# The right operands of a seven-product down projection, formed during the up projection and kept in DRAM

## Chip, cores and metric

The kernel runs on one core of one Trainium2 chip. The metric is device time in microseconds: the median of three runs of the kernel is 1607.43 us (1604.57 to 1608.24). Lower is better.

## What is computed

One layer of an encoder over 1024 prompt tokens and 32 sample tokens: a modulated input projection, two groups of attention heads, an output projection with a norm, and then a feed-forward part with a norm. The change lies in the feed-forward part, which the reference writes as

```python
def _conv_ffn(u, conv_prev, w_up, conv_w, conv_b, w_down):
    T = u.shape[1]
    a, b = jnp.split(jnp.einsum('btd,df->btf', u, w_up), 2, axis=-1)
    a_pad = jnp.concatenate([conv_prev.astype(a.dtype), a], axis=1)
    conv = conv_b
    for j in range(CONV_WIDTH):
        conv = conv + a_pad[:, j:j + T] * conv_w[j]
    h = jax.nn.silu(conv) * b
    return jnp.einsum('btf,fd->btd', h, w_down), a_pad[:, -(CONV_WIDTH - 1):]
```

with u of 1024 features, h of 2816 (22 tiles of 128) and everything in float32.

## The kernel before

**Exact products.** TensorE multiplies float32r. `split` (L87 to L89) makes two float32r parts of a float32 tile: `hi` by a copy on ScalarE (ACT) and `lo`, the difference, on VectorE (DVE) or GpSimd (POOL). `mm3` (L82) then does three matmuls for one product.

**Up projection.** The loop over `j` (22 tiles of h) and `s` (gate half, plain half) takes 44 units. A unit loads 512 KB of `w_up` (`up_weights`, L868, on SyncE's queue, SP), splits it (tiles `wu`, two buffers each of raw, hi and lo), and does 144 matmuls of 352 columns into three accumulators. With `s == 0` ACT copies the accumulators to `row` and DVE does the convolution (L1129 to L1131) and ACT the SiLU; with `s == 1` DVE multiplies into `hT[j]` (L1137 to L1139). The buffers of `wu` are free for unit u + 2 when TensorE (PE) has done unit u. A generator `residuals` (L1081 to L1105), advanced once in each unit, turns the rows that the first norm left in DRAM into the residual of the second: SP loads a piece of `dx1`, POOL multiplies and adds, POOL stores it to `dres`; a piece has `RW` = 256 columns, so there are 36.

**Down projection.** h (1024 by 2816) times `w_down` (2816 by 1024) is done as a two by two block product with seven products of half size instead of eight (sums of blocks on both sides). Products are `i` = 0 to 6, each with 11 steps `k`, so 77 steps `n`; a step is 4 blocks of 128 tokens with 3 matmuls each of 128 by 512, and four of the products carry the 32 sample tokens with 2 more matmuls a step: 924 + 88 = 1012 matmuls. For a step the kernel does three things ahead: `load(n + 3)` brings one or two 256 KB tiles of `w_down`; `left(n)` sums tiles of h for later products; `prepare(n + 2)` forms the left operand (from h) and the right operand (from `w_down`), the sums mostly on POOL (L1198, L1211, L1216, L1218, L1220, L1226), and splits both into `hi` and `lo` (tiles `oh`, `ol`, four buffers, shared in turn by two pools). Both need DVE's subtraction on L89. In products 5 and 6 the finished rows get their gate and residual on POOL (L1258, L1259, 128 by 1024) and their norm on ACT and DVE.

**Order.** Most of this is ordered by the framework's scheduler. Each engine, and SP's queue, then takes its instructions strictly in that order.

Of the kernel before, what the change touches and what calls it, by code (L numbers as in the profile page):

```python
# [16 lines left out]
P = 128  # L17
# [10 lines left out]
TT = T + TS  # L28
# [7 lines left out]
RW = 256  # L36
# [17 lines left out]
def layer_kernel(ctx: ExitStack, tc: tile.TileContext, a: dict, o: list):  # L54
# [88 lines left out]
    dres = dp.tile([TT, D], F32, name="dres")  # L143

# [928 lines left out]
    hT = [hpool.tile([P, TT], F32, name=f"h{j}") for j in range(NJ)]  # L1073
    with pool("pe") as pe:
# [31 lines left out]
        resid = residuals()  # L1106
        for j in range(NJ):
            c = pe.tile([P, ROW], F32, name=f"cv{j}", tag="cv", bufs=1)
            for s in range(2):
                if j or s:  # L1110
                    next(resid, None)
# [40 lines left out]
    NK = NJ // 2  # L1152
# [3 lines left out]
    with pool("px") as px, pool("pf") as pf:  # L1156
# [10 lines left out]
        res, ready, raws_, rest = {}, {}, {}, []  # L1167
# [3 lines left out]

        def wq(fh, ch, k):
            return w_dn[:, fh * NK + k, ch * 512:(ch + 1) * 512]


        LOADS = [((1, 0), None), ((1, 1), None), ((0, 1), (0, 0)), ((0, 0), None), (None, (1, 1)), ((1, 1), (0, 1)), (None, (1, 0))]

        def load(n):
            if n >= NPH * NK:
                return  # L1180
            i, k = divmod(n, NK)
            raw = (px.tile if n % 3 == 2 else pw.tile)([P, 2, 512], F32, name=f"xt{i}{k}", tag="raw", bufs=1 if n % 3 == 2 else 2)
            x2 = None
            if LOADS[i][0]:
                nc.sync.dma_start(raw[:, 1], wq(*LOADS[i][0], k))
            if LOADS[i][1]:
                x2 = pt_(f"x2{i}{k}", "x2", 3, (P, 512))
                nc.sync.dma_start(x2, wq(*LOADS[i][1], k))
            raws_[n] = raw, x2

        def left(n):

            if n >= NPH * NK:
                return
            i, k = divmod(n, NK)
            if i == 0:
                nc.vector.tensor_tensor(xq[k], hq(0, 1, k), hq(1, 1, k), ALU.add)
                nc.gpsimd.tensor_tensor(xq[k], xq[k], hq(0, 0, k), ALU.subtract)  # L1198

        def prepare(n):  # L1200
# [4 lines left out]
            raw, x2 = raws_.pop(n)  # L1205
            pl = px if n % 4 < 2 else pw
            hi = pl.tile([P, 2, 512], F32R, name=f"oh{i}{k}", tag="wh", bufs=2)
            lo = pl.tile([P, 2, 512], F32R, name=f"ol{i}{k}", tag="wl", bufs=2)
            yk = hq(1, 0, k)
            if i == 1:  # L1210
                nc.gpsimd.tensor_tensor(raw[:, 0], hq(1, 0, k), xq[k], ALU.subtract)  # L1211
                split(hi, lo, raw)
            else:
                if i == 2:
                    nc.vector.tensor_tensor(raw[:, 0], hq(0, 1, k), hq(1, 1, k), ALU.add)
                    nc.gpsimd.tensor_tensor(yk, raw[:, 1], x2, ALU.subtract)  # L1216
# [20 lines left out]
            ready[n] = hi, lo  # L1237
# [153 lines left out]

    hp_.__exit__(None, None, None)
# [61 lines left out]
```

## Time and profile before

| | us |
|---|---|
| median of 3 runs | 1607.43 |
| the profiled execution, its own time | 1607.87 |
| span in the profile | 1606.1 |
| PE busy | 1493.1 (93%) |
| DVE busy | 884.0 (55%) |
| POOL busy | 563.9 (35%) |
| up projection, about | 784 to 1299 |
| down projection, first to last matmul, about | 1300 to 1578 |
| end after the last matmul | about 28 |

Busy time is the time in which an engine worked on an instruction; a matmul's end is modelled, so that PE's busy time is not PE at its peak. In the page's 40 slices the down projection is slices 33 to 39. A wait is put down to what ended it. The DMA share is the mean busy share of the core's 16 DMA engines; it can go a little over 1 where transfers of several queues overlap.

### The profile page before, as it was taken

The page shows a single profiled execution, that of the slowest core. Times are in us where ns is not written, and L with a number is a line of the kernel's source. Part 1 is how long each engine was busy: PE and PEld are TensorE (multiplying, and loading weights), DVE is VectorE, ACT ScalarE, POOL GpSimd, SP SyncE. Part 2 cuts the span into 40 slices and gives each one's busy share as a digit, 9 for nine tenths or more (in the row PEclk, how much of TensorE's full clock was granted, in tenths as well). Part 3 has the DMA queues.
Part 4 walks back from the last instruction along what each step waited for, and adds up shares of the span by engine and source line. Part 5 has one row for each costly group of instructions (what it writes and reads, how often), then busy time and mean ns, then how long its engine had stood idle before and what let it go on. Part 6 is the DMA issues. An engine that isn't in the chain of part 4 may idle for free.

```text
span 1606.1 us, 22667 instructions
## 1 busy us (share of the span) xinstructions
PE 1493.1 (93%) x8525; PEld 1242.7 (77%) x8525; DVE 884.0 (55%) x1621; ACT 575.5 (36%) x1176; POOL 563.9 (35%) x635
## 2 busy tenths in 40 slices
PE   6999999978999999899999999999999999999753
PEld 4677777745546777687899999999999987878542
DVE  4522336644446899467753243323332378797996
ACT  3211211245647787535532112111211134444321
POOL 0002014644413433124355650000000056583885
PEclk9999999999999999999999999999999999999977
DMA  9623411489653444335423331111111122543322
GB/s 267 164 94 110 130 47 69 146 235 255 179 179 91 122 108 95 137 133 208 143 76 108 105 109 51 53 40 53 40 53 40 40 80 87 168 154 116 133 81 78
DMA packets 177967, 183.86 MB, mean 114 GB/s; under 512 B 9121, under 2 KB 138178, under 8 KB 177858
## 3 DMA queue, kind: packets, MB, share of 16 engines
q1 hardware_dynamic: 167858, 151.00, 31.6%
q0 software_dynamic: 9424, 30.37, 6.4%
q8 instruction: 67, 1.10, 0.3%
q10 hardware_dynamic: 576, 1.05, 0.2%
q14 instruction: 42, 0.34, 0.1%
HBM read 147.62 MB, written 26.38 MB: 108 GB/s over the span
## 4 chain that ended last, share of the span: by engine, by line
PE 65%; DVE 12%; DMA 10%; POOL 5%; issue 4%; SPq 2%; ACT 2%; POOLq 0%; DVEq 0%; ACTq 0%
PE up L82 15%; PE upc L82 8%; PE wd L82 7%; PE wo L82 4%; DVE ol L89 3%; PE po L82 3%; PE Sf L82 2%; DMA dres<-rr 2%; PE ptf L116 2%; DMA rr<-dx 2%; PE Sd L82 2%; DMA adan<-in_w_ada 1%; PE pod L82 1%; DMA xt<-in_w_down 1%; POOL rr L1099 1%
## 5 line engine op out<-in xcount | busy, mean ns | idle before, releaser
L82 PE MATMUL wd<-ol,oh 128*128 128x512 f32 x308 | 119.9, 403 | 17.9 <-DVE ol L89 17.9
L82 PE MATMUL wd<-oh,ol 128*128 128x512 f32 x308 | 119.5, 403 | 6.8 <-DVE ol L89 6.7
L82 PE MATMUL wd<-oh 128*128 128x512 f32 x308 | 114.0, 397 | 4.9 <-ACT oh L88 2.4
L1127 POOL COPY cvo<-row 128x2 f32<-128x2 f32 x22 | 15.5, 706 | 277.2 <-ACT row L1125 277.2
L89 DVE TENSOR_TENSOR ol<-h,oh 128x512 fp32r<-128x512 f32 x77 | 80.9, 1064 | 25.3 <-ACT oh L88 24.9
L628 POOL TENSOR_SCALAR wf<-wf,rs 128x128 f32<-128x128 f32 (+7 forms) x64 | 47.4, 745 | 109.3 <-DVE rs L594 81.7
L82 PEld LDWEIGHTS wd<-ol,oh 128*128 128x128 f32 x308 | 59.3, 193 | 33.8 <-DVE ol L89 21.6
L82 PEld LDWEIGHTS wd<-oh,ol 128*128 128x128 f32 x308 | 59.6, 194 | 22.8 <-DVE ol L89 10.8
L82 PEld LDWEIGHTS wd<-oh 128*128 128x128 f32 x308 | 59.0, 192 | 19.5 <-ACT oh L88 2.8
L88 ACT CAST oh<-h 128x512 fp32r<-128x512 f32 x77 | 46.7, 618 | 70.9 <-PE wd L82 30.6
L1124 ACT COPY row<-up 128x352 f32<-128x352 f32 x44 | 17.8, 458 | 142.0 <-PE up L82 112.2
L1132 ACT ACTIVATE cv<-cv 128x1058 f32<-128x1058 f32 x22 | 24.0, 1089 | 103.5 <-DVE cv L1131 103.5
L89 DVE TENSOR_TENSOR ol<-xt,oh 128x512 fp32r<-128x512 f32 (+1 forms) x55 | 54.8, 999 | 8.2 <-ACT oh L88 8.2
L88 ACT CAST oh<-xt 128x512 fp32r<-128x512 f32 (+1 forms) x55 | 38.8, 707 | 54.7 <-PE wd L82 31.3
L593 ACT ACTIVATE wf<-wf,lo 128x128 f32<-128x128 f32 (+7 forms) x64 | 49.5, 776 | 23.4 <-DVE lo L590 21.5
L89 DVE TENSOR_TENSOR wh<-wr,wh 128x512 fp32r<-128x512 f32 x40 | 28.6, 738 | 51.2 <-ACT wh L88 51.2
L82 PE MATMUL po<-ptpf,vf 128*64 128x256 f32 (+1 forms) x320 | 54.8, 378 | 0.5 <-DVE ptpf L618 0.4
L88 ACT CAST wh<-wr 128x512 fp32r<-128x512 f32 x40 | 24.3, 621 | 86.0 <-DMA wr<-in_w_in 19.0
L593 ACT ACTIVATE wd<-wd,lo 128x128 f32<-128x128 f32 (+7 forms) x64 | 49.6, 777 | 13.0 <-DVE lo L590 11.0
L590 DVE CUSTOM_DVE_ANT_0 wf<-Sf,nb 128x512 f32<-128x512 f32 (+3 forms) x64 | 36.9, 588 | 31.1 <-PE Sf L82 19.7
L653 POOL TENSOR_SCALAR wd<-wd,rs,lam 128x128 f32<-128x128 f32 (+7 forms) x32 | 26.5, 827 | 63.0 <-DVE rs L594 57.8
L116 PE MATMUL ptf<-cst,wf 128*128 128x128 f32 x288 | 47.1, 284 | 1.1 <-POOL wf L628 0.7
(1542 smaller groups left out, 4823.2 us busy)
## 6 DMA issues: line engine op xcount, KB each, us to landing
xt<-in_w_down SPq DMA_DIRECT2D x55, 256.0 KB
x<-in_w_down SPq DMA_DIRECT2D x44, 256.0 KB
wr<-in_w_in SPq DMA_DIRECT2D x20, 512.0 KB
adam<-in_w_ada SPq DMA_DIRECT2D x32, 256.0 KB
adan<-in_w_ada SPq DMA_DIRECT2D x32, 256.0 KB
ga<-in_w_ada SPq DMA_DIRECT2D x16, 512.0 KB
out<-z POOLq DMA_DIRECT2D x12, 512.0 KB, 4.0
x<-in_x_prompt SPq DMA_DIRECT2D x8, 512.0 KB
```

The source lines that it names most:

```text
L82: nc.tensor.matmul(out, l, r, start=start, stop=stop, **k)
L88: nc.scalar.copy(hi, src)
L89: (eng or nc.vector).tensor_tensor(lo, src, f(hi), ALU.subtract)
L116: nc.tensor.transpose(out, in_, ident[:n, :n])
L590: nc.vector.tensor_tensor_reduce(w[:, c], S[:, 0:n], t, -1.0, lo, ALU.add, ALU.min, lo_)
L593: nc.scalar.activation(w[:, 0:ext], w[:, 0:ext], AF.Exp, bias=lo, scale=-1.0, accum_out=sm)
L628: nc.gpsimd.tensor_scalar(w, w, rs, 1.0, ALU.mult, ALU.mult)
L653: nc.gpsimd.tensor_scalar(e1, e1, r1, lam, ALU.mult, ALU.mult)
L1099: nc.gpsimd.tensor_tensor(r, r, gb[c0][0:n, 0], ALU.mult)
L1124: nc.scalar.copy(row[:, 2 + g * G3:2 + (g + 1) * G3], accs[g])
L1127: nc.gpsimd.tensor_copy(cvo[:, 0, :, j], row[:, T:T + 2])
L1132: nc.scalar.activation(c[:, 0:L], c[:, 0:L], AF.Silu)
```

## The change

The right operands of the seven products (sums of tiles of `w_down`, and their `hi` and `lo`) are formed by a generator during the first tiles of the up projection and stored to DRAM in `dwn` (154 tiles of 128 by 512, 40.4 MB). The down projection loads them ready made. The generator is advanced three times in each unit of `j` < 16; its tiles live where the last six tiles of h will be. The sums of h that POOL did go to DVE. The residual pieces get half as wide (128 columns, so 72), and two are taken per unit.

```diff
-RW = 256
+RW = 128
...
+    dwn = dp.tile([7 * NJ, P, 512], F32, name="dwn")
...
+    LENT = 6
+    hT = [hpool.tile([P, TT], F32, name=f"h{j}") for j in range(NJ - LENT)]
+    lent_ = pool("ln", "right")
...
+    def right_operands():
+        q = {}
+        def load(k, which):
+            for fh, ch in which:
+                q[k, fh, ch] = t = lent.tile([P, 512], F32, name=f"wq{k}{fh}{ch}", tag=f"wq{fh}{ch}", bufs=1)
+                nc.sync.dma_start(t, w_dn[:, fh * NK + k, ch * 512:(ch + 1) * 512])
+        late = []
+        def stored(due):
+            while late and (due is None or late[0][0] <= due):
+                _, i, k, hl = late.pop(0)
+                for p in range(2):
+                    nc.sync.dma_start(dwn[(i * NK + k) * 2 + p], f(hl[p]))
+        n = 0
+        load(0, ((0, 0), (0, 1), (1, 1), (1, 0)))
+        yield
+        for k in range(NK):
+            t = lent.tile([P, 512], F32, name=f"wt{k}", tag="wt", bufs=1)
+            for i, src in ((3, "00"), (2, "t1"), (5, "t3"), (4, "t2"), (1, "11"), (6, "t4"), (0, "10")):
+                stored(n - 2)
...
+                if src == "t1":
+                    nc.vector.tensor_tensor(t, q[k, 0, 1], q[k, 0, 0], ALU.subtract)
...
+                hl = [lent.tile([P, 512], F32R, name=f"wn{i}{k}{p}", tag=f"wn{p}", bufs=4) for p in range(2)]
+                split(hl[0], hl[1], x)
+                late.append((n, i, k, hl))
+                n += 1
+                yield
...
         for j in range(NJ):
+            if j == NJ - LENT:
+                for _ in operands:
+                    pass
+                lent_.__exit__(None, None, None)
...
-                if j or s:
+                for _ in range(2 if j or s else 0):
                     next(resid, None)
...
+                    if j < NJ - LENT:
+                        next(operands, None)
...
         def load(n):
...
+            hi = pl.tile([P, 2, 512], F32R, name=f"oh{i}{k}", tag="wh", bufs=2)
+            lo = pl.tile([P, 2, 512], F32R, name=f"ol{i}{k}", tag="wl", bufs=2)
+            for p, t in enumerate((hi, lo)):
+                nc.sync.dma_start(f(t[:, 1]), dwn[(i * NK + k) * 2 + p])
...
-                nc.gpsimd.tensor_tensor(xq[k], xq[k], hq(0, 0, k), ALU.subtract)
+                nc.vector.tensor_tensor(xq[k], xq[k], hq(0, 0, k), ALU.subtract)
...
-                split(hi[:, 1], lo[:, 1], r)
-                split(hi[:, 0], lo[:, 0], l)
-                if i == 3:
-                    nc.gpsimd.tensor_tensor(l, l, hq(0, 1, k), ALU.subtract)
+            split(hi[:, 0], lo[:, 0], l)
+            if i == 3:
+                nc.vector.tensor_tensor(l, l, hq(0, 1, k), ALU.subtract)
```

**DVE in the up projection**, from the split of the weights of `j` = 3 on (`wu30l`; `cv` is the convolution, `h` the product with the plain half). Before:

```order
L89 TENSOR_TENSOR wu30l_8424<-wu30r_8421,wu30h_8423 128x1024
L1129 TENSOR_SCALAR cv2_8227<-row2_8313,cvw_67,pcol_66 128x1058
L1130 SCALAR_TENSOR_TENSOR cv2_8227<-row2_8313,cvw_67,cv2_8227 128x1058
L1131 SCALAR_TENSOR_TENSOR cv2_8227<-row2_8313,cvw_67,cv2_8227 128x1058
L1137 TENSOR_TENSOR h2_7843<-up21_8337,cv2_8227 128x352 x2
L1138 TENSOR_TENSOR h2_7843<-upc21_8338,cv2_8227 128x320
```

and of the change (`wn` are the new operands, named by product, k and part; `wt` a sum of tiles of `w_down`):

```order
L89 TENSOR_TENSOR wu30l_8591<-wu30r_8588,wu30h_8590 128x1024
L1199 TENSOR_SCALAR cv2_8327<-row2_8443,cvw_67,pcol_66 128x1058
L89 TENSOR_TENSOR wn521_8546<-wq201_8350,wn520_8545 128x512
L1200 SCALAR_TENSOR_TENSOR cv2_8327<-row2_8443,cvw_67,cv2_8327 128x1058
L89 TENSOR_TENSOR wn421_8600<-wt2_8478,wn420_8599 128x512
L1201 SCALAR_TENSOR_TENSOR cv2_8327<-row2_8443,cvw_67,cv2_8327 128x1058
L1121 TENSOR_TENSOR wt2_8478<-wq210_8511,wt2_8478 128x512
L89 TENSOR_TENSOR wn121_8634<-wq211_8413,wn120_8633 128x512
L1207 TENSOR_TENSOR h2_7844<-up21_8476,cv2_8327 128x352 x2
L89 TENSOR_TENSOR wn621_8665<-wt2_8478,wn620_8664 128x512
L1208 TENSOR_TENSOR h2_7844<-upc21_8477,cv2_8327 128x320
```

The operands' subtractions and sums now stand between the convolution and the products, and the next split of `wu` behind them: from `wu30l` to `wu90l` there are 56 of the 77 steps, so 9.3 in each `j`, and the last of the 77 stands just ahead of `wu91l`.

**SP's queue** at the same place, from the load of `wu30r` on. Before:

```order
L868 DMA wu30r_8421<-in_w_up 128x8x128
L1091 DMA rr05_8419<-dx1_83 128x256
L1091 DMA rr06_8517<-dx1_83 128x256
L1091 DMA rr07_8607<-dx1_83 128x256
L1091 DMA rr08_8705<-dx1_83 32x256
L868 DMA wu31r_8519<-in_w_up 128x8x128
```

and of the change, its first rows:

```order
L869 DMA wu30r_8588<-in_w_up 128x8x128
L1095 DMA dwn_85<-wn000_8138 128x512
L1095 DMA dwn_85<-wn310_8169 128x512
L1095 DMA dwn_85<-wn601_8107 128x512
L1095 DMA dwn_85<-wn001_8139 128x512
L1087 DMA wq110_8230<-in_w_down 128x512
L1095 DMA dwn_85<-wn311_8170 128x512
L1087 DMA wq200_8348<-in_w_down 128x512
L1095 DMA dwn_85<-wn210_8233 128x512
L1151 DMA rr04_8213<-dx1_83 128x128
```

Between the loads of `wu30r` and `wu31r` there are 19 transfers now, where there were four; every store among them is queued behind those ahead of it and waits for the ACT or DVE result that it stores.

**DVE in the down projection**, from the second step of product 4 on. Before:

```order
L89 TENSOR_TENSOR ol41_13146<-h12_7853,oh41_13145 128x512
L89 TENSOR_TENSOR ol41_13146<-xq0_12003,oh41_13145 128x512
L89 TENSOR_TENSOR ol42_13182<-h13_7854,oh42_13181 128x512
L1373 TENSOR_TENSOR ya0_11995<-ya0_11995,wd30_12888 128x512
L89 TENSOR_TENSOR ol42_13182<-xq1_12004,oh42_13181 128x512
```

and of the change:

```order
L89 TENSOR_TENSOR ol41_13852<-xq0_12812,oh41_13851 128x512
L89 TENSOR_TENSOR ol42_13872<-xq1_12813,oh42_13871 128x512
L1420 TENSOR_TENSOR ya0_12804<-ya0_12804,wd30_13640 128x512
```

Of the two subtractions of a step one is left.

## Rows read from the trace of the kernel before

**Rows 1.** The page's head and part 1: busy time of the engines.
```profile
span 1606.1 us, 22667 instructions
...
PE 1493.1 (93%) x8525; PEld 1242.7 (77%) x8525; DVE 884.0 (55%) x1621; ACT 575.5 (36%) x1176; POOL 563.9 (35%) x635
```

**Rows 2.** Busy time by stage: window, PE, PEld, DVE, ACT, POOL, PEclk, DMA, GB/s.
```profile
1299.00:1342.00 43.00, 40.30 (x170) 30.73 (x168) 39.14 (x51) 16.22 (x38) 35.95 (x16) 1.00 0.32 105
...
784.00:1299.00 515.00, 511.07 (x3200) 508.60 (x3199) 186.07 (x234) 111.29 (x181) 114.06 (x207) 1.00 0.22 66
1299.00:1472.00 173.00, 167.28 (x723) 134.17 (x722) 146.23 (x186) 75.39 (x156) 102.88 (x59) 1.00 0.40 133
1472.00:1579.00 107.00, 79.97 (x299) 58.87 (x297) 106.14 (x111) 28.95 (x53) 83.35 (x42) 0.89 0.29 101
1579.00:1606.10 27.10, 0.00 (x0) 0.00 (x0) 13.73 (x28) 3.15 (x4) 18.75 (x17) 0.58 0.22 82
```

**Rows 3.** The chain that ended last, in order of time: start, us, what.
```profile
1276.34 7.63 PE up L82 x48
1283.97 3.81 PE upc L82 x24
...
1299.85 1.21 DVE ol L89 x2
...
1342.17 19.58 PE wd L82 x85
...
1413.04 58.82 PE wd L82 x258
```

**Rows 4.** Waits of PE from 1298 us on: us in total, times, longest.
```profile
PE wd L82 <- DVE ol L89: 24.6, 13, 9.8
```

**Rows 5.** Groups of instructions from 1298 us on: busy us, mean ns, idle before.
```profile
L1218 POOL TENSOR_TENSOR h<-x,h 128x512 f32<-128x512 f32 x22 | 38.0, 1744 | 1.8 <-DMA x<-in_w_down 1.6
L1198 POOL TENSOR_TENSOR xq<-xq,h 128x512 f32<-128x512 f32 x11 | 28.7, 2642 | 5.6 <-DVE xq L1197 5.6
L89 DVE TENSOR_TENSOR ol<-xt,oh 128x512 fp32r<-128x512 f32 x44 | 39.7, 903 | 2.8 <-ACT oh L88 2.8
```

**Rows 6.** Groups of DVE from 1470 to 1580 us, the same columns.
```profile
L89 DVE TENSOR_TENSOR ol<-h,oh 128x512 fp32r<-128x512 f32 x32 | 36.9, 1185 | 0.0
L1274 DVE TENSOR_TENSOR ya<-ya,lng 128x1024 f32<-128x1024 f32 x4 | 8.2, 2055 | 0.0
```

**Rows 7.** Tile ol: duration ns min/median/max, first and last start us.
```profile
L89 DVE TENSOR_TENSOR ol<-h,oh x77: 668/684/2875, 1288.3 to 1568.8; 128x512 fp32r<-128x512 f32 x77
```

**Rows 8.** Tile yb on POOL, the same columns.
```profile
L1259 POOL TENSOR_TENSOR yb<-yb,rs x4: 2497/2808/2835, 1552.8 to 1569.3; 128x1024 f32<-128x1024 f32 x4
L1315 POOL TENSOR_TENSOR yb<-yb,lnb x4: 1257/1260/1265, 1592.8 to 1601.6; 128x512 f32<-128x512 f32 x4
```

**Rows 9.** Tile wu100h, the weights of unit j = 10, s = 0.
```profile
L82 PE MATMUL up<-u2h,wu100h x16: 320/323/325, 1024.3 to 1031.5; 128*128 128x352 f32 x16
...
L89 DVE TENSOR_TENSOR wu100l<-wu100r,wu100h x1: 1225/1225/1225, 1014.0 to 1014.0; 128x1024 fp32r<-128x1024 f32 x1
```

**Rows 10.** Busy time in stretches of interest for the DMA, columns as in rows 2.
```profile
20.00:60.00 40.00, 35.07 (x254) 23.28 (x253) 23.27 (x46) 16.53 (x28) 0.00 (x0) 1.00 1.08 282
1362.00:1413.00 51.00, 48.19 (x207) 38.25 (x205) 41.32 (x49) 22.80 (x46) 32.36 (x21) 1.00 0.52 171
1395.00:1405.00 10.00, 10.00 (x45) 7.89 (x43) 8.85 (x6) 4.33 (x8) 9.78 (x7) 1.00 0.61 199
194.00:198.00 4.00, 4.00 (x19) 3.31 (x18) 1.98 (x3) 2.14 (x4) 0.00 (x0) 1.00 1.03 397
1000.00:1200.00 200.00, 200.00 (x1260) 200.00 (x1259) 63.64 (x78) 38.61 (x62) 11.20 (x34) 1.00 0.16 46
940.00:960.00 20.00, 18.20 (x101) 17.34 (x100) 6.42 (x7) 3.90 (x7) 12.68 (x23) 0.91 0.44 131
```

**Rows 11.** SP's queue at the start of the up projection: start, us, what.
```profile
788.44 0.37 SPq L868 DMA_DIRECT2D wu11r<-in_w_up  x1
```

More of the change, by code (lines that the diff above doesn't have):

```diff
@@ L1072, in layer_kernel @@
     hpool = hp_.__enter__()
-    hT = [hpool.tile([P, TT], F32, name=f"h{j}") for j in range(NJ)]
+    NK = NJ // 2
+    LENT = 6
+    hT = [hpool.tile([P, TT], F32, name=f"h{j}") for j in range(NJ - LENT)]
+    lent_ = pool("ln", "right")
+    lent = lent_.__enter__()
+    def right_operands():
[17 more added lines that the diff above has]
+                stored(n - 2)
+                if k + 1 < NK:
+                    if i == 1:
+                        load(k + 1, ((0, 0), (0, 1)))
+                if k and i == 2:
+                    load(k, ((1, 0),))
+                if i == 0 and k + 1 < NK:
+                    load(k + 1, ((1, 1),))
+                if src == "t1":
+                    nc.vector.tensor_tensor(t, q[k, 0, 1], q[k, 0, 0], ALU.subtract)
+                    x = t
+                elif src == "t3":
+                    x = q[k, 0, 1]
+                    nc.vector.tensor_tensor(x, q[k, 1, 1], x, ALU.subtract)
+                elif src == "t2":
+                    nc.vector.tensor_tensor(t, q[k, 1, 1], t, ALU.subtract)
+                    x = t
+                elif src == "t4":
+                    nc.vector.tensor_tensor(t, q[k, 1, 0], t, ALU.subtract)
+                    x = t
+                else:
+                    x = q[k, int(src[0]), int(src[1])]
+                hl = [lent.tile([P, 512], F32R, name=f"wn{i}{k}{p}", tag=f"wn{p}", bufs=4) for p in range(2)]
[3 more added lines that the diff above has]
+                yield
+        stored(n - 2)
+        yield
+        stored(None)
@@ L1106, in layer_kernel @@
         resid = residuals()
+        operands = right_operands()
         for j in range(NJ):
+            if j == NJ - LENT:
+                for _ in operands:
+                    pass
+                lent_.__exit__(None, None, None)
+                hp2_ = pool("h2", "right")
+                hpool2 = hp2_.__enter__()
+                hT += [hpool2.tile([P, TT], F32, name=f"h{i}") for i in range(j, NJ)]
             c = pe.tile([P, ROW], F32, name=f"cv{j}", tag="cv", bufs=1)
             for s in range(2):
-                if j or s:
+                for _ in range(2 if j or s else 0):
                     next(resid, None)
@@ L1151, in layer_kernel @@
     psum("psd", m=6, po=1, ms=1)
-    NK = NJ // 2
     NPH = 7
@@ L1181, in load @@
             i, k = divmod(n, NK)
[L1182 to L1189, printed above, removed]
+            pl = px if n % 4 < 2 else pw
+            hi = pl.tile([P, 2, 512], F32R, name=f"oh{i}{k}", tag="wh", bufs=2)
+            lo = pl.tile([P, 2, 512], F32R, name=f"ol{i}{k}", tag="wl", bufs=2)
+            for p, t in enumerate((hi, lo)):
+                nc.sync.dma_start(f(t[:, 1]), dwn[(i * NK + k) * 2 + p])
+            ready[n] = hi, lo
         def left(n):
-            if n >= NPH * NK:
-                return
             i, k = divmod(n, NK)
```

33 lines of the change are left out of this document (10 added, 23 removed).

## The prediction, made before the changed kernel ran

> **What bounds the kernel now.** I read the page's head first: PE is busy for 93% of the span, so time comes back only where PE is held up, and is lost wherever PE is held up anew [rows 1]. The busy time by stage shows where. In the up projection PE works for 511 of 515 us while DVE works for 186, POOL for 114 and the DMA engines at a share of 0.22: PE sets the pace, and the others have room. In the down projection it turns round: from 1472 to 1579 us DVE is busy for 106 of 107 us, PE for 80 at a granted clock of 0.89 [rows 2]. The chain of waits gives PE's own pace where nothing holds it: 258 matmuls of the down projection take 58.8 us, 0.228 us each; a unit of the up projection takes 7.63 + 3.81 = 11.4 us, so a tile j of h takes 22.9 us [rows 3]. PE's largest wait in the down projection is for DVE's subtraction that makes `ol`: 24.6 us in 13 waits [rows 4].
>
> So the down projection could take 1012 x 0.228 = 231 us. It takes from 1299.85 [rows 3] to 1579, 279 us. **48 us are lost**: some 4 in the first 43 us (170 matmuls are 39 us of work), some 39 after 1472 us (about 300 matmuls are 68 us of work in 107), the rest, 5, between [rows 2, 3].
>
> **The change, part by part.**
>
> *Down projection, DVE and POOL.* Gone are 55 of the 132 subtractions of `ol`, in the trace 0.90 us each for the 44 of them that have rows of their own, and all 77 sums on POOL, of which the two largest groups alone take 38.0 and 28.7 us [rows 5]. To DVE come 33 of these sums (products 0 to 3), at 0.684 us, the median of a subtraction of that size [rows 7]: 23 us. In the late stage the subtractions of `ol` take 1.19 us on average, not 0.684, and the scaling of a finished row 2.06 us [rows 6, 7], where a subtraction of the same width takes 1.23 alone [rows 9]: they stretch when POOL works at the same time. What POOL keeps there are 16 operations of 128 by 1024, 2.5 us each at the least [rows 8], 40 us. DVE keeps 22 subtractions, 8 scalings and 8 sums of 512 columns. Unstretched that is 22 x 0.684 + 8 x 1.23 + 8 x 0.684 = 30 us. If the two engines never overlapped, it would be 70 us beside PE's 68. So DVE and PE come out about even. I leave 6 us of loss for the strict order of DVE there; the bounds are 0 and 20, half of what is lost now. With the 4 us at the start, where DVE still has sums to do first, 10 of 48 us stay: **-38 us**.
>
> *Down projection, transfers.* A step now loads two tiles of 256 KB, 0.52 MB in 13.1 x 0.228 = 3.0 us, 175 GB/s. The products before moved 171 GB/s at a share of 0.52 [rows 10], so the engines can carry it. The load for step n + 3 starts when PE is done with step n - 1 (four buffers), three steps or 9 us ahead of its use. I cost this at nothing; PE's steps in between are the cover, and without it PE would wait for each landing.
>
> *Up projection, DVE.* Seven steps need 7 subtractions and 4 sums, 11 operations at 0.684 us. In order, 9.3 steps stand in each j until all 77 are done, a little under j = 10: 10.0 us for each j, on top of 63.6 us in 200 or 7.3 us in 22.9 [rows 10]. That is 17.3 of 22.9 us, hidden as long as nothing that DVE waits for is late. ACT gets 9.3 copies for each j and is busy for 111 of 515 us now [rows 2]: hidden.
>
> *Up projection, transfers.* This is the step that can cost. 9.3 steps are 9.3 x (2 stores + 4/7 load) x 0.262 = 6.3 MB; with the weights (1.05 MB, 512-byte pieces) and about three residual pieces in and out (0.4 MB), 7.7 MB for each j. The prices lie far apart. Loads of 2 KB pieces moved 171 GB/s at a share of 0.52, so 329 at a share of 1; the best stretch of such pieces moved 397 at 1.03; the weights moved 46 at 0.16, so 288 [rows 10]. At full share that is 6.3 / 0.329 + 1.45 / 0.288 = 24.1 us, or 20.8 us with 397, against PE's 22.9. No row shows full share with a queue in which each store waits for an engine, so I take 92% of the lower price, 26 us: 329 is of `w_down` itself, the very rows that are moved, and of 51 us, not 4. Why it reaches PE: DVE takes its instructions in order, the split of the weights for j + 1 stands behind the operands, and an operand needs one of four buffers, so the store of four steps before must have landed. The cover is that the split of the weights is done at 1015.2 where PE needs it at 1024.3 [rows 9]: 9.1 us. From `wu30l` to `wu91l` there are 61 steps, 6.6 j, so the delay is 6.6 x (26 - 22.9) - 9.1 = **+11 us**, with bounds of 0 (20.8 us for each j) and the slow case below. The 16 steps before `wu30l` have from 788.4 us, when the last load ahead of them was issued [rows 11], until j = 3 at about 864, 75 us for 11 MB; they cost nothing.
>
> A rule speaks against this step. The Trainium skill, "DMA: Bandwidth & Descriptors", section "Bandwidth", wants transfers of 1 MiB or more for 75% of peak, and lists 138 GB/s for 64 KB and 341 for 1 MB; the operands go in 256 KB. Between the two I would estimate 240 GB/s by that page, 32 us for each j, and the sum would be 13 us above the time before instead of below it. The trace does not quite bear it out: transfers of mostly 256 KB moved 282 GB/s over 40 us, several in flight [rows 10].
>
> *Residuals.* 72 pieces of half the width move the same bytes. POOL is busy for 114 of 515 us [rows 2], so nothing; bounds: 0 and the 2 us that PE lost once from 940 to 960 us [rows 10], when these pieces were done and weights were late. *The end* after the last matmul, 27 us of POOL and DVE [rows 2], is the same code; 0.
>
> **Sum** against the profiled execution's 1607.87 us: -38 + 11 = -27, so 1581 us. That execution stands 0.4 us above the median of the runs, 1607.43, which changes nothing.
>
> **Rivals.**
> *The up projection hides it all.* If 2 KB pieces move at the 397 GB/s of the best stretch, j takes 20.8 us of transfers and the delay is 0: 1570 us. For it: shares over 1 in two rows of four. Against: those stretches had no waiting stores.
> *The up projection becomes bound by the transfers, and it gets slower.* The mechanism is SP's strict order: a store waits for its result, and loads that DVE needs next wait behind it. The best 10 us of `w_down` loads moved 199 GB/s at 0.61 [rows 10], in a queue that also waited on engines. It decides from a delay of 38 us on, 30 us for each j, 257 GB/s. At 230 GB/s j takes 33.5 us and the delay is 61: 1631 us. The rule above would put it here too, at 1621.
> *The late down projection stays bound by DVE and POOL.* If half of the 48 us stays, because finished rows and splits still block each other in order, it is -24 + 11: 1595 us. For it: the stretch to 2.06 us [rows 6]; against: of POOL's sums in that stage the half of L1218's that belongs to product 6, 19 us [rows 5], is gone, and L1220's with it.
> That the change does not do what it says can be set aside: in order DVE has 77 subtractions of `ol` left.
>
> **How the numbers follow.** The forecast (1572 to 1600) gets 0.48; all hidden 0.22; slower by transfers 0.13; DVE and POOL bound 0.12; the rest, between the last two and near no change, 0.05. The forecast's own bounds, 6 us of loss being 0 to 20 and a delay of 0 to 30, reach 1564 to 1614, and from 1564 to 1612 holds all but the slow case and a little on the fast side. About 0.2% (3 us) can be told from no change. Faster 0.82, same 0.05, slower 0.13.
>
> **What would show it.** Right: PE busy from about 1310 us without the gaps of now, a down projection of 235 to 245 us, `ol` in 77 instructions, DVE well under full there; in the up projection gaps in PE from j = 4 to j = 10, each ended by a split of `wu`, behind it stores or loads, and none after j = 10; a DMA share near 1 from about 850 to 1020 us. Wrong: no gaps in the up projection (all hidden), or waits of PE on `wu` that sum to over 38 us, or PE in the late down projection still waiting for `ol` for more than 20 us, or for landings of `oh` and `ol`.

## The result and the profile after

The changed kernel takes **1580.46 us** (median of four runs, 1580.09 to 1583.7) against 1606.99 us of the kernel before in the same comparison: a ratio of **0.9841, interval 0.9824 to 0.9859**, 26.5 us less. The forecast was 1581 us. The sum was right, but three of its terms were not, in both directions. The page of the changed kernel, first its span and busy times, then the shares of the chain that ended last, for [rows 1]:

```profile
span 1578.6 us, 23523 instructions
PE 1487.8 (94%) x8525; PEld 1243.1 (79%) x8525; DVE 866.0 (55%) x1709; ACT 580.9 (37%) x1187; POOL 479.0 (30%) x670
PE 73%; DMA 10%; DVE 7%; POOL 3%; issue 3%; SPq 2%; ACT 1%; POOLq 0%; DVEq 0%; ACTq 0%
```

POOL's busy time fell from 563.9 us to 479.0, DVE's only from 884.0 to 866.0, since the up projection took over work. By stage (columns as in [rows 2]: us, busy time of PE, PEld, DVE, ACT and POOL, clock, DMA share, GB/s):

```profile
784.00:1299.00 515.00, 510.18 (x3185) 507.54 (x3184) 259.98 (x355) 153.64 (x256) 166.63 (x316) 0.99 0.50 167
1299.00:1342.00 43.00, 40.11 (x181) 32.93 (x180) 28.48 (x62) 12.53 (x34) 0.39 (x3) 1.00 0.51 165
1342.00:1450.00 108.00, 108.00 (x478) 89.43 (x477) 51.04 (x105) 32.12 (x70) 0.00 (x0) 1.00 0.57 182
1450.00:1551.00 101.00, 91.50 (x379) 69.69 (x377) 79.52 (x100) 22.85 (x40) 50.99 (x24) 0.98 0.62 212
1551.00:1578.00 27.00, 0.00 (x0) 0.00 (x0) 14.57 (x26) 3.14 (x4) 16.97 (x17) 0.53 0.22 83
```

From 1342 to 1450 us PE is busy for 108 of 108 us, where DVE now works for 51. PE is idle at the two ends: 2.9 us from 1299 to 1342, ahead of the first matmul of the down projection, and 9.5 us from 1450 to 1551; the 27 us after the last matmul are as before. The chain of waits says the same: one piece of 780 matmuls at 0.227 us each, where [rows 3] had pieces of 85 and 258, and after it waits for DVE and landings, of which the longest is shown:

```profile
1304.88 177.39 PE wd L82 x780
1513.44 20.55 PE wd L82 x89
1534.36 4.57 DMA ol<-dwn
```

PE's waits from 1300 us on, for [rows 4] (us in total, times, longest); the 24.6 us for `ol` have become 1.7:

```profile
PE wd L82 <- DMA oh<-dwn: 6.5, 3, 4.2
PE wd L82 <- DVE wds L89: 1.8, 2, 1.5
PE wd L82 <- DVE ol L89: 1.7, 1, 1.7
```

Set out by the first matmul of the up projection, the first and the last of the down projection, and the end of the span, the profiled executions of all kernels divide as follows (us; "up" runs to the first matmul of the down projection, so it holds the wait between the two):

| kernel | up | down | end | median | ratio to before, interval |
|---|---|---|---|---|---|
| before | 515.3 | 278.9 | 27.4 | 1606.99 | |
| changed | 520.5 | 245.5 | 28.2 | 1580.46 | 0.9841, 0.9824 to 0.9859 |
| e1, four residual buffers | 513.6 | 251.2 | 28.2 | 1576.78 | 0.9793, 0.9765 to 0.9822 |
| e2, wide residual pieces | 514.0 | 248.9 | 25.8 | 1576.40 | 0.9795, 0.9766 to 0.9824 |
| e3, late residual loads by POOL | 522.4 | 248.4 | 31.3 | 1587.59 | 0.9859, 0.983 to 0.9888 |
| e4, sums of h on POOL | 520.5 | 255.3 | 28.9 | 1591.50 | 0.9888, 0.9859 to 0.9917 |
| e5, a third store | 522.4 | 248.3 | 28.2 | 1589.69 | 0.9881, 0.9849 to 0.9914 |
| e6, gate on DVE | 521.4 | 248.4 | 21.8 | 1578.89 | 0.9812, 0.9788 to 0.9835 |
| e7, wide pieces and gate | 514.4 | 249.9 | 19.4 | 1568.68 | 0.9745, 0.9722 to 0.9769 |
| e8, and the end on DVE | 514.3 | 249.6 | 17.0 | 1570.19 | 0.9760, 0.9737 to 0.9783 |
| e9, pieces of 512 bytes | 538.2 | 249.1 | 28.2 | 1600.48 | 0.9948, 0.9925 to 0.997 |
| e10, before, gate on DVE | 514.4 | 272.9 | 24.2 | 1598.16 | 0.9939, 0.9918 to 0.9959 |
| e11, e7 and signs on ACT | 514.1 | 237.6 | 23.8 | 1563.07 | 0.9712, 0.9681 to 0.9744 |

So the down projection gave 33.4 us, and the up projection with the step to the down projection took 5.2 us back: 0.8 more at the end leaves 27.4 of the span. PE's own pace would be 231 us for the down projection; 14.5 us are still lost in it, all of them in the last 232 matmuls, which take 68.3 us (92.1 before). Each row is one profiled execution, so small differences need care. Changed, e1, e2, e5 and e9 run the same operations in the same order on every engine in this stage: their last 232 matmuls took 68.3 to 69.4 us, but their first 100 took 23.1 to 27.6, with a granted clock that differed there (see e1, e2).

### The profile page after: what moved, and what is told of

It is laid out like the page before. It is cut to its first block, busy times and chain, and to the rows that moved or that the text cites. A ratio compares the mean times of both kernels' runs of the same rounds, so it can differ in the third digit from the quotient of the medians.

```text
span 1578.6 us, 23523 instructions
## 1 busy us (share of the span) xinstructions
PE 1487.8 (94%) x8525; PEld 1243.1 (79%) x8525; DVE 866.0 (55%) x1709; ACT 580.9 (37%) x1187; POOL 479.0 (30%) x670
## 3 DMA queue, kind: packets, MB, share of 16 engines
q10 hardware_dynamic: 576, 1.05, 0.2%
## 4 chain that ended last, share of the span: by engine, by line
PE 73%; DMA 10%; DVE 7%; POOL 3%; issue 3%; SPq 2%; ACT 1%; POOLq 0%; DVEq 0%; ACTq 0%
PE up L82 16%; PE wd L82 13%; PE upc L82 8%; PE wo L82 4%; PE po L82 3%; PE Sf L82 2%; DMA dres<-rr 2%; DMA rr<-dx 2%; PE ptf L116 2%; PE Sd L82 2%; PE pod L82 1%; DMA adan<-in_w_ada 1%; SPq L175 1%; POOL rr L1160 1%; DMA wrfq<-in_w_in 1%
## 5 line engine op out<-in xcount | busy, mean ns | idle before, releaser
L1159 POOL TENSOR_TENSOR rr<-rr,gb 128x128 f32<-128x128 f32 (+1 forms) x72 | 44.1, 614 | 97.0 <-DMA rr<-dx 96.6
L1305 POOL TENSOR_TENSOR ya<-ya,g2p 128x1024 f32<-128x1024 f32 x4 | 10.3, 2580 | 170.8 <-DVE ya L1427 170.2
L89 DVE TENSOR_TENSOR ol<-h,oh 128x512 fp32r<-128x512 f32 x44 | 41.4, 956 | 32.7 <-ACT oh L88 32.7
L594 ACT ACTIVATE wf<-wf,lo 128x128 f32<-128x128 f32 (+7 forms) x64 | 49.5, 776 | 18.0 <-DVE lo L591 15.8
L88 ACT CAST oh<-h 128x512 fp32r<-128x512 f32 x44 | 27.1, 620 | 75.4 <-PE wd L82 61.1
L1160 POOL TENSOR_TENSOR rr<-rr,gb 128x128 f32<-128x128 f32 (+1 forms) x72 | 47.1, 655 | 5.0
```

The costliest lines, as they stand in the source:

```text
L88: nc.scalar.copy(hi, src)
L89: (eng or nc.vector).tensor_tensor(lo, src, f(hi), ALU.subtract)
L594: nc.scalar.activation(w[:, 0:ext], w[:, 0:ext], AF.Exp, bias=lo, scale=-1.0, accum_out=sm)
L1159: nc.gpsimd.tensor_tensor(r, r, gb[c0][0:n, 0], ALU.mult)
L1160: nc.gpsimd.tensor_tensor(r, r, gb[c0][0:n, 1], ALU.add)
```

## Where the time goes in the up projection

The transfers did not delay PE. Two stretches of the changed kernel by stage, the stage of the operands and the one gap that is left:

```profile
820.00:1000.00 180.00, 180.00 (x1133) 180.00 (x1132) 139.83 (x196) 80.01 (x133) 60.54 (x105) 1.00 0.98 346
1120.00:1140.00 20.00, 17.43 (x90) 16.69 (x89) 1.84 (x2) 3.31 (x6) 10.41 (x25) 0.83 0.32 94
```

For 180 us the DMA engines move 346 GB/s at a share of 0.98, and PE is busy for 180.00 of them. The gap of before from 940 to 960 us [rows 10] is gone, some 4 us gained. But from 1120 to 1140 us PE is idle for 2.6 us and its granted clock is 0.83 on average; counted by when the tiles start, j = 12 to 16 cost 6.4 us. The operands are stored by then. What SP does just there (start, duration in the queue):

```profile
1104.83 0.38 SPq L869 DMA_DIRECT2D wu140r<-in_w_up  x1
1106.03 14.54 SPq L1151 DMA_DIRECT2D rr<-dx  x4
1120.67 0.39 SPq L869 DMA_DIRECT2D wu141r<-in_w_up  x1
```

Between the loads of `wu140r` and `wu141r` lie 15.8 us, of which four loads of residual pieces take 14.5; a unit of PE takes 11.4. Each of these loads needs the buffer of two pieces back, and waits until that piece's store has landed. SP's largest wait, in the changed kernel from 998 to 1160 us,

```profile
SPq L1151 <- DMA dres<-rr: 127.1, 43, 8.7
```

and in the kernel before while it moved most of its 36 pieces of twice the width, 820 to 998 us:

```profile
SPq L1091 <- DMA dres<-rr: 114.9, 32, 7.3
```

That is 3.0 us a wait for pieces of 128 columns and 3.6 us for pieces of 256 (4.2 us in e2, below): **a piece costs SP a round trip, and half the width saves only a small part of it**, and the change doubled the pieces.

**e1, e2.** Two edits that take this away, one by more buffers, one by undoing the narrowing:

```diff
-r = pe.tile([P, RW], F32, name=f"rr{c0}{b}", tag="rr", bufs=2)
+r = pe.tile([P, RW], F32, name=f"rr{c0}{b}", tag="rr", bufs=4)
```
```diff
-RW = 128
+RW = 256
-                for _ in range(2 if j or s else 0):
+                for _ in range(1 if j or s else 0):
```

> The changed kernel with four buffers instead of two for a residual piece; nothing else differs. Theory (the round trip of a piece): SP waits 127 us from 998 to 1160 us for stores of residual pieces to land, 43 times, because a piece's load needs the buffer of two pieces back; so it issues the weights of a unit 15 us apart instead of 11.4, and PE loses 6.4 us from 1120 to 1140 us. With four buffers the waits fall below 60 us, the weights are issued ahead of need, the gap is gone, and the kernel takes about 1574 us. Rival 1 (POOL's two operations and the bandwidth set a piece's pace): the waits stay near 120 us and the time at 1580. Rival 2 (the cover was already used up by the transfers of the operands until 1000 us): a gap of 2 to 6 us comes earlier, between 1000 and 1060 us, and the time is 1577 to 1580.

> The narrowing of the residual pieces undone: 36 pieces of 256 columns, one for each unit, as before the change; all else as in the changed kernel. Theory (a piece costs SP a round trip whatever its width, about 3.3 us): half as many pieces take half of SP's time, the gap from 1120 to 1140 us (6.4 us) goes, the up projection ends about 1295 instead of 1301.6, and the kernel takes about 1574 us. Rival (bytes, not pieces, set the pace): the same waits, the same gap, 1580 us. My recorded forecast priced the narrowing at 0 with bounds of 0 and 2 us.

Both took about 4 us less than the changed kernel (1576.78 and 1576.40 us; of the intervals of the ratios one just misses and one just touches that of the changed kernel). SP's wait from 998 to 1160 us in e2, and the stretch with the gap (e1: 40.6 us in 17 waits, PE 20.00 of 20 too):

```profile
SPq L1151 <- DMA dres<-rr: 45.8, 11, 8.1
```
```profile
1120.00:1140.00 20.00, 20.00 (x128) 20.00 (x127) 7.38 (x9) 3.88 (x6) 1.27 (x4) 1.00 0.18 53
```

The gap is gone, and the stage "up" falls from 520.5 us to 513.6 and 514.0, as the theory had it; bytes are the same, so the rival of e2 falls. The whole gains less than 6.5 us because in both the down projection took 3.4 to 5.7 us more. Most of that lies in its first 100 matmuls: 27.6 us in e1 and 25.8 in e2 against 23.1 in the changed kernel. The same 25 us from its start on, in the changed kernel, e1 and e2:

```profile
1304.90:1329.90 25.00, 25.00 (x109) 20.40 (x110) 19.85 (x42) 4.96 (x14) 0.00 (x0) 1.00 0.54 176
1295.70:1320.70 25.00, 23.65 (x89) 18.63 (x90) 18.49 (x38) 3.58 (x11) 0.00 (x0) 0.86 0.37 122
1298.10:1323.10 25.00, 24.95 (x97) 20.04 (x98) 19.21 (x40) 4.22 (x12) 0.00 (x0) 0.87 0.43 148
```

In e1 and e2 the granted clock stood at 0.50, its lower level (1.2 GHz), from 1297.6 to 1304.4 us; e1 also waited 1.3 us for a landing of `ol`. PE had been without a matmul of the two projections for 3.2 to 3.3 us just before in all three, so why the clock fell in only two of them no run here shows.

**e5.** To press on the transfers, each step stores the first part of its operand a second time:

```diff
+                nc.sync.dma_start(dwx[i * NK + k], f(hl[0]))
```

> The changed kernel with a third store of 256 KB for each step of the operand stage: the first part of every operand is stored a second time, into memory that nobody reads. A tile j then moves 9.3 x 0.262 = 2.4 MB more, some 10.1 MB instead of 7.7. Theory A (transfers near their limit, about 350 GB/s at a share of 1, are what paces the stage once they exceed PE's 22.9 us): 28.9 us for each j, 6 us more than PE over 6.6 to 8 tiles, so PE loses 25 to 45 us from 850 to 1040 us, each gap ended by a split of wu, at a share of 1; the kernel takes 1605 to 1625 us. Theory B (the rate still rises when more transfers are in flight, or the weights' cover takes it): PE loses under 5 us, 1580 to 1585 us. My recorded forecast had the transfers at 26 us for each j already without the extra store.

1589.69 us (its up projection began 4.6 us later than that of the changed kernel, ahead of anything that the edit touches, so the stages tell more than the time), and neither theory in its form. PE has no gap while the operands are stored; the storing goes on longer instead, to 1065 us:

```profile
940.00:980.00 40.00, 40.00 (x253) 40.00 (x253) 25.11 (x37) 15.17 (x27) 8.94 (x17) 1.00 1.00 346
840.00:1060.00 220.00, 220.00 (x1385) 220.00 (x1385) 138.73 (x193) 79.18 (x136) 53.60 (x96) 1.00 1.00 354
```

The rate is near that of the changed kernel: 354 GB/s, over 220 us at a share of 1.00. So 346 was near the most that a whole stage of these transfers moved in any run here. But the edit did not keep the order: between two splits of `wu` on DVE now stand mostly three or four splits of operands, in the changed kernel four or five. The extra bytes were spread over more tiles, and the residual pieces came later, with their gap (4.1 us for `wu190h`) behind them. So this run shows the rate and not the coupling.

**e9.** The coupling shows where the order stays and the price rises. Each operand is kept as four blocks of 128 by 128, so that its stores and loads go in pieces of 512 bytes:

```diff
-    dwn = dp.tile([7 * NJ, P, 512], F32, name="dwn")
+    dwn = dp.tile([7 * NJ, 4, P, 128], F32, name="dwn")
-nc.sync.dma_start(dwn[(i * NK + k) * 2 + p], f(hl[p]))
+nc.sync.dma_start(dwn[(i * NK + k) * 2 + p].rearrange("c p d -> p c d"), f(hl[p]).rearrange("p (c d) -> p c d", c=4))
```

> The changed kernel with each operand of 256 KB kept in memory as four blocks of 128 by 128, so that its stores and its loads go in pieces of 512 bytes instead of 2 KB; the order of the instructions on DVE, ACT and PE is the same one, and SP's too but for these shapes. The weights, in pieces of 512 bytes, moved 46 GB/s at a share of 0.16, 288 GB/s at a share of 1. At that price a tile j takes 6.3 / 0.288 + 1.4 / 0.35 = 26 us, just the price of my recorded forecast, against 22.9 of PE. Theory A (the recorded coupling: DVE's strict order carries each late store over to the splits of wu, with 9.1 us of cover): PE loses 8 to 14 us between 900 and 1040 us, in waits for splits of wu, and 1590 to 1597 us in all. Theory B (late stores do not reach PE within the stage, because there is more cover than I took): no gap until 1000 us, the stage of the operands ends some 20 us later, and SP's delay shows in larger gaps from 1000 to 1160 us, 1580 to 1588 us. Theory C (pieces of 512 bytes cost the queues more than the weights' row says): a rate under 250 GB/s, gaps of 30 us or more, over 1610 us. In the down projection 175 GB/s are wanted, a share of 0.6: no more waits than before under A and B.

1600.48 us, 20 more than the changed kernel. The stretch with the first gap, PE's waits in the up projection, and DVE's largest wait from 820 to 1080 us:

```profile
900.00:940.00 40.00, 35.29 (x204) 34.71 (x204) 26.61 (x36) 16.03 (x29) 9.40 (x20) 0.91 1.04 306
1000.00:1020.00 20.00, 18.59 (x115) 18.01 (x114) 13.65 (x19) 8.15 (x15) 6.08 (x13) 1.00 1.04 311
```
```profile
PE up L82 <- DVE wu60l L89: 3.8, 1, 3.8
PE up L82 <- DVE wu90l L89: 1.4, 1, 1.4
PE up L82 <- DVE wu50l L89: 0.9, 1, 0.9
```
```profile
DVE wn L89 <- DMA dwn<-wn: 49.5, 31, 4.6
```

and DVE just before the split that PE waited for longest:

```profile
930.83 0.69 DVE L89 TENSOR_TENSOR wn<-wt,wn 128x512 fp32r<-128x512 f32 x1 [4.63 <-DMA dwn<-wn]
932.64 1.22 DVE L89 TENSOR_TENSOR wu60l<-wu60r,wu60h 128x1024 fp32r<-128x1024 f32 x1
```

Here is the recorded chain, link by link: DVE's split of an operand waits for a store to land (31 times, 49.5 us; in the changed kernel 14 times, 22.9 us, without a gap in PE), the split of `wu60` stands behind it, and PE waits for that. By its matmuls (0.158 us each, 254 in 40 us) PE loses 50 of them, 7.9 us, in the first row and 13, 2.0 us, in the second; part of this is the granted clock, 0.91 in the first row. That is the 8 to 14 us of theory A, though not by its sum: the rate was 306 to 317 GB/s, a tile takes 7.7 / 0.311 = 24.8 us and not 26, and 6.6 x (24.8 - 22.9) - 9.1 is 3.4 us. So the cover was less than the 9.1 us that I took, or the late stores bunch; that was not tried apart. Later, where SP is late between residual pieces, j = 12 to 15 cost 14.2 us by when the tiles start, against 6.4 in the changed kernel: theory B's part, on top, and together more than either theory's time. (A share over 1 takes no second queue, other than said ahead of the prediction: in the stretch of 1.08 in [rows 10] one queue alone stood at 107.9%.)

## Where the time goes in the late down projection

**e3.** The landings that PE waits for there are of loads that SP issued late: SP takes its orders strictly, and in the changed kernel loads of residual rows (L1295) wait 22.8 us for POOL. So POOL issues them itself:

```diff
-            nc.sync.dma_start(res[b][0:rows(b)], dres[b * P:b * P + rows(b)])
+            nc.gpsimd.dma_start(res[b][0:rows(b)], dres[b * P:b * P + rows(b)])
```

> The changed kernel with the loads of finished residual rows in the late down projection issued by POOL, which also uses them, instead of SP; stores of finished rows stay with SP. Theory (SP's strict order): operand tiles that are queued behind a residual load that waits for POOL land on time, PE's waits for landings of oh and ol (6.5 us in the late stage) fall to about half, and the gap from 1520 to 1550 us shrinks by 4 to 6 us: about 1575 us. Rival 1 (DVE and POOL together set the pace there, DVE is busy for 19.8 of 20 us): PE's waits move from landings to DVE's subtractions and the time stays within 2 us of 1580. Rival 2 (POOL now waits for each residual row itself, 2 to 3 us each, and its operations in the last product come later): the end moves out, 1582 to 1588 us.

1587.59 us, 7 us more than the changed kernel, though the intervals of the ratios overlap (0.9830 to 0.9888 against 0.9824 to 0.9859). PE's waits from 1300 us on:

```profile
PE wd L82 <- DVE ol L89: 5.8, 2, 4.0
PE wd L82 <- DVE yb L1423: 3.0, 1, 3.0
PE wd L82 <- DMA oh<-dwn: 1.6, 1, 1.6
```

The landings did fall, from 6.5 us to 1.6, and waits for DVE took their place: 5.8 and 3.0. The last 232 matmuls took 69.0 us, no less than with SP's loads. The trace bears out the mechanism of the first rival in that stage and that of the second at the end, which went from 28.2 us to 31.3. SP's order was a link, not the bound.

**What DVE does there.** DVE in the changed kernel, then POOL (start, duration):

```profile
1479.71 2.38 DVE L89 TENSOR_TENSOR wds<-sa,wds 128x32 fp32r<-128x32 f32 x1
1482.12 2.28 DVE L1282 TENSOR_SCALAR sa<-h 128x32 f32<-128x32 f32 x1
1487.73 0.18 DVE L89 TENSOR_TENSOR wds<-sa,wds 128x32 fp32r<-128x32 f32 x1
1487.94 0.18 DVE L1282 TENSOR_SCALAR sa<-h 128x32 f32<-128x32 f32 x1
```
```profile
1479.19 5.17 POOL L1305 TENSOR_TENSOR ya<-ya,g2p 128x1024 f32<-128x1024 f32 x2
1484.33 2.93 POOL L1306 TENSOR_TENSOR ya<-ya,rs 128x1024 f32<-128x1024 f32 x1
```

An operation on 128 by 32 takes 2.38 us and 2.28 us while POOL multiplies, and 0.18 us when POOL has done its last at 1487.3. DVE gets one operation in for each of POOL's. The Trainium skill, "SBUF — State Buffer", section "SBUF: two separate sides", says that the two engines share a pair of ports as an exclusive lock, which the one that starts first holds for a whole instruction (on DVE's side for operations in a two-port mode or with two inputs in SBUF). The trace agrees in that DVE's operation stands still for one of POOL's: 2.3 us for what takes 0.18.

**e6, e7, e8.** So the gate and the residual of the finished rows go from POOL to DVE, alone (e6), with the wide pieces of e2 (e7), and with POOL's operations of the end too (e8):

```diff
-            nc.gpsimd.tensor_tensor(y, y, consts["g2p"], ALU.mult)
-            nc.gpsimd.tensor_tensor(y, y, res[b], ALU.add)
+            nc.vector.tensor_tensor(y, y, consts["g2p"], ALU.mult)
+            nc.vector.tensor_tensor(y, y, res[b], ALU.add)
```
```diff
-            nc.gpsimd.tensor_tensor(y[:, C1], y[:, C1], consts["lng"][:, C1], ALU.mult)
+            nc.vector.tensor_tensor(y[:, C1], y[:, C1], consts["lng"][:, C1], ALU.mult)
...
```

> The changed kernel with the 16 operations of 128 by 1024 that POOL does on finished rows in the late down projection (times the gate, plus the residual) done by DVE instead; nothing else differs. Theory (DVE and POOL stand still for each other there: a DVE operation of 128 by 32 takes 2.38 us when POOL works and 0.18 when not): DVE gets 16 x 1.22 = 20 us of its own work and loses some 30 us of standing still, SP's waits for POOL (22.8 us) go, PE loses 3 to 8 us instead of some 13 from 1480 to 1551 us, and the kernel takes 1570 to 1576 us. Rival (DVE is simply full from 1480 to 1520 us, and 20 us more of work delay the splits further): PE loses 20 us or more in waits for ol and wds, 1586 to 1595 us.

> Both of the mends together: residual pieces of 256 columns as before the change, and the gate and residual of the late down projection on DVE. Theory (two separate losses, one in the up projection, one in the late down projection): the gains add, about 6 us from the first and what the gate on DVE alone gives from the second: 1564 to 1571 us. Rival (the late down projection gives back what comes earlier): no more than the better of the two, 1573 to 1576 us.

> The same, and in the end after the last matmul also POOL's 8 operations of 128 by 512 on DVE. Theory (the two engines stand still for each other at the end too: DVE operations of 128 by 512 take up to 2.3 us there, 0.6 to 0.7 alone): the end falls from 27 us to about 20, so 6 to 8 us less than the kernel without this: 1557 to 1564 us. Rival (DVE's chain of finished rows sets the end, and 8 x 0.66 = 5 us more of it come on top): the end 30 us or more, 3 to 5 us slower than without it.

e6 took 1578.89 us, and its interval overlaps that of the changed kernel: alone, the edit can't be told from none. In e7 it nearly can be, 1568.68 against 1576.40 us of e2 (the intervals overlap by 0.0003). But not in the way I expected, PE losing 3 to 8 us where it lost 13. No operation of DVE is stretched any more, yet the down projection takes as long as without the edit or longer (248.4 and 249.9 us, the last 232 matmuls 70.0 and 71.5), and the gain lies at the end: 21.8 and 19.4 us instead of 28.2 and 25.8. Within the down projection PE's waits only changed their name, in e7:

```profile
PE wd L82 <- DMA oh<-dwn: 9.2, 5, 3.2
PE wd L82 <- DMA ol<-dwn: 1.0, 2, 0.7
```

The loads that land late are issued when PE lets go of a buffer, and PE holds a step's buffers until the step's small products of the sample have run. Those wait for splits of `wds`, and these stand behind gate operations (L1305) in DVE's order. Pieces of the chain of waits in e7 that show it:

```profile
1509.34 2.35 DVE yb L1305 x2
1511.69 0.11 DVE wds L89
1511.85 0.75 PE wd L82 x2
1512.79 5.68 DMA ol<-dwn
```

That this order sets the time is a reading so far; e11 tries it. e8 shortened the end by 2.4 us more in the profile, but its time is that of e7, above the 1557 to 1564 us expected: its up projection began 3.5 us later, in code that none of these edits touch, so 2.4 us are not shown.

**e11.** The 11 changes of sign from which these splits are made go from DVE to ACT, on top of e7:

```diff
-nc.vector.tensor_scalar(x, hT[k][:, T:TT], -1.0, None, ALU.mult)
+nc.scalar.activation(x, hT[k][:, T:TT], AF.Identity, scale=-1.0)
```

> The version with wide residual pieces and the gate on DVE, with the 11 changes of sign of the sample's h in the sixth product moved from DVE to ACT. In that version PE loses 7 to 9 us from 1500 to 1520 us in waits for landings whose loads wait for PE: a step's buffers are held until its small sample products have run, and those wait for splits of wds that stand in DVE's order behind gate operations. Theory: with the signs ready early the splits move forward in the order, buffers come free earlier, PE loses 3 to 5 us less: 1562 to 1567 us. Rival (DVE is full in that product, about 44 us of work for 33 us of PE): no change, 1567 to 1570 us.

1563.07 us, and the down projection 237.6 us instead of 249.9. PE's chain is nearly whole, and its waits for `oh` from 1300 us on are 0.3 us:

```profile
1298.53 207.67 PE wd L82 x900
```
```profile
L89 DVE TENSOR_TENSOR wds<-sa,wds x22: 168/185/193, 1330.7 to 1503.3; 128x32 fp32r<-128x32 f32 x22
```

900 matmuls run in one piece: the splits of `wds` come earlier in DVE's order. The last of them now stands ahead of the gate operations on `yb` (in e7 the last, at 1520.90 us, stands behind all eight of these):

```profile
1503.28 0.19 DVE L89 TENSOR_TENSOR wds<-sa,wds 128x32 fp32r<-128x32 f32 x1
1506.99 2.35 DVE L1305 TENSOR_TENSOR yb<-yb,g2p 128x1024 f32<-128x1024 f32 x2
```

The row of the splits of `wds` (shortest, median and longest in ns) ends at 193 ns, as in e7; in the changed kernel, with POOL's wide operations, the longest was 2387. The down projection gained 12 us in the profile, and its last 232 matmuls 15 (56.4 us against 71.5), more than the 3 to 5 expected. The 11 operations that left DVE took some 2 us in all, so it was mainly the order of DVE's work that PE waited for and not its amount; the end gave 4.4 back (23.8 us). The time, 1563.07 us, lies 5.6 under e7, with intervals that overlap, so against e7 alone the gain of the whole is not shown; against the changed kernel they lie well apart (0.9744 at most, 0.9824 at least). This version beats both kernels.

**e4.** The other half of the change, undone alone: the 33 sums of h go back to POOL.

```diff
-                nc.vector.tensor_tensor(xq[k], xq[k], hq(0, 0, k), ALU.subtract)
+                nc.gpsimd.tensor_tensor(xq[k], xq[k], hq(0, 0, k), ALU.subtract)
...
-                    nc.vector.tensor_tensor(l, hq(1, 0, k), xq[k], ALU.subtract)
+                    nc.gpsimd.tensor_tensor(l, hq(1, 0, k), xq[k], ALU.subtract)
...
-                nc.vector.tensor_tensor(l, l, hq(0, 1, k), ALU.subtract)
+                nc.gpsimd.tensor_tensor(l, l, hq(0, 1, k), ALU.subtract)
```

> The second part of the change undone alone: the 33 subtractions of h by xq and the like in products 0, 1 and 3 go back from DVE to POOL; the operands still come from memory. Theory (in products 0 to 3 PE sets the pace, DVE has room for 23 us): the same time, 1579 to 1583 us, PE at 0.227 us a matmul through the middle. Rival (POOL and DVE stretch each other, which the change to DVE alone removed): subtractions of ol in the middle go from about 0.69 us to 0.9 us or more, PE waits there for ol or for sums on POOL by 5 to 15 us in all, 1586 to 1596 us.

1591.50 us, 11 more (the intervals of the ratios just touch), as the rival had it, but not in its place. By stage, and PE's largest wait from 1299 to 1342 us:

```profile
1299.00:1342.00 43.00, 31.80 (x128) 25.74 (x128) 30.34 (x35) 7.42 (x22) 22.73 (x17) 0.84 0.36 117
1342.00:1450.00 108.00, 108.00 (x478) 89.42 (x477) 46.53 (x85) 32.16 (x71) 24.52 (x19) 1.00 0.55 176
```
```profile
PE wd L82 <- DVE wds L89: 8.1, 1, 8.1
```

In the middle PE still works for 108 of 108 us. The loss is in the first 43 us, where both engines have sums to make at once: splits of `wds` take up to 1.28 us there, in the changed kernel 0.19 at the most. One wait of 8.1 us is most of it; the rest is the granted clock, 0.84 in that stretch. The first 100 matmuls took 35.0 us against 23.1, the last 232 some 2 less than in the changed kernel. So the second part of the change is worth some 10 us in the down projection, all at the start.

**e10.** Was it the gate on POOL that held the kernel before up? The edit of e6, made in the kernel before:

```diff
-            nc.gpsimd.tensor_tensor(y, y, consts["g2p"], ALU.mult)
+            nc.vector.tensor_tensor(y, y, consts["g2p"], ALU.mult)
...
```

> The kernel before the change, with only the gate and the residual of the late down projection moved from POOL to DVE; the sums of the operands stay on POOL. Theory (in that stage what costs is every operation of POOL, about 2.4 us of DVE's time each; 16 gate operations are 44 us, 18 sums 32 us): DVE stands still for 44 us less and works for 16 x 1.2 = 20 us more, so PE's loss of 39 us after 1472 us falls to 12 to 25 us, and the kernel takes 1580 to 1595 us, near what the whole change gave. Rival (the sums of the operands on POOL set the pace there, so only the change as made helps): 1603 to 1610 us. Second rival (DVE is full with its own work): slower, 1610 to 1622 us.

1598.16 us: 0.6% less than before, just outside the range of the theory. The down projection falls from 278.9 us to 272.9 and the end from 27.4 to 24.2, and PE still waits 10.7 us for `ol` and 7.0 for ACT's copies. So the gate on POOL cost the kernel before some 9 us, 6 of them in the down projection. The change left the gate on POOL and still took 33 us off that projection, so these came from the sums and subtractions that left POOL and DVE; how much from each was not tried apart, but for the sums of h (e4).

## Why the prediction came out, point by point

- **Down projection, -38 us.** Right in its mechanism: PE's pace through the middle, 24.6 us of waits for `ol` down to 1.7. It measured -33.4 us from first to last matmul, and the step into it took 2.7 more (3.3 us between the up projection's last matmul and the next one, 0.6 before: the first operand's load waits on SP until the convolution state has been read): -30.7. The term that was mis-sized is the loss I left: 10 us, of which 6 late. It was 14.5 + 3.3 us. DVE and POOL do take turns, as that sum had it; but I took 6 us "for the strict order of DVE there" out of bounds of 0 and 20, and between the profiles of e7 and e11 that order was worth 12. The 30 us of DVE's own work were too few as well: in e7, where nothing in that stage is stretched, DVE is busy for 69.7 us from 1465.5 to 1549.2 us, 50 without the 16 gate operations of 1.2 us. The sum left out the norm's statistics, the sample's operations and some of the sums.
- **Transfers of the down projection, 0.** The cover of three steps held in the middle and failed late: 6.5 us of landings, which the prediction had named as a sign of being wrong. I had said that PE would wait for each landing without the cover, and not asked what takes it away: a load issued late, behind another on SP (e3) or behind a buffer that a small product holds (e7, e11).
- **Up projection, transfers, +11 us.** Wrong; 0, and "no gaps in the up projection" was among the prediction's own signs of being wrong. The failing step is the price, "I take 92% of the lower price, 26 us". Measured were 346 GB/s at a share of 0.98, so 7.7 / 0.346 = 22.3 us for each j, under PE's 22.9 (21.8 at the 354 GB/s of e5). A queue whose stores wait for an engine reached full share all the same. The rival that hides it all was right here in its outcome, though not by its 397 GB/s. The coupling itself was right, and at the price of e9 it appeared where the prediction put it, at j = 5, 6 and 9, ended by splits of `wu`; but its sum gives 3.4 us there where some 10 were lost.
- **The rule against the step.** The Trainium skill, "DMA: Bandwidth & Descriptors", section "Bandwidth", led me to estimate 240 GB/s for transfers of 256 KB. This trace does not bear out that estimate: 346 GB/s, with loads and stores of mostly that size side by side. The page's table is of loads issued from GpSimd, and these transfers were issued by SyncE.
- **Residuals, 0 with bounds of 0 and 2.** Wrong. I counted bytes and POOL's time; the cost was SP's round trip, 72 times instead of 36. It made a new gap of 6.4 us, while the old one of 4 us went: +2.5 for the stage. e2 puts the narrowing at 6.5 us of the up projection.
- **The end, 0.** 0.8 us.

So the transfers cost 11 us less than forecast; the residuals 2.5, the down projection with its start 7.3 and the end 0.8 us more, 10.6 together. The errors cancelled: that 1581 met 1580.46 so closely was luck, with a mechanism that was right for the down projection and two terms that were wrong for the up projection.

## What to carry to other kernels

Count what a queue does in trips, not in bytes: where a load waits for a store of its own buffer, halving the piece doubles the trips at nearly the same cost each (3.0 us against 3.6 here), and what stands behind it on that queue pays. Where DVE is near full, a wide POOL operation beside it cost DVE about its own length here (2.3 us); moving it onto DVE can be the cheaper way, and work on DVE that a scarce buffer waits for must stand ahead of work that nobody waits for. Look at the granted clock before a difference of a few us is given a cause. And a sum that comes out right is no proof of its terms: look at each stage by itself.

## What was not expected of the hardware

- DVE and POOL keep each other out for whole operations, even small ones: 0.18 us became 2.38 us; without POOL's wide operations the longest of 22 such splits took 193 ns (e7 and e11).
- Stores and loads of 256 KB in pieces of 2 KB moved 346 GB/s over 180 us at a share of 0.98, while PE was busy for 180.00 of the 180 us at a granted clock of 1.00; with the stores and part of the loads in pieces of 512 bytes (e9) it was 306 to 317 at a share of 1.04 to 1.05.
- A residual piece held its queue for 3.0 us a wait at 128 columns and 3.6 to 4.2 us at 256.
- The same instructions in the same order took 23.1 to 27.6 us for the first 100 matmuls of the down projection in five profiled executions, after a gap of some 3 us in each: the granted clock of the 25 us from its start was 0.86 (e1), 0.87 (e2), 0.88 (e9), 0.93 (e5) and 1.00 (changed).
